# A dilated 3x3 convolution on one core: the first pair's load in one transfer, the later loads asked for five pairs ahead

## The chip, the core and the metric

The kernel runs on one core of one Trainium2 chip. The metric is device time in microseconds (us) of one execution. A measurement of this kernel repeats to about 1%: three runs of the kernel before lie between 126.32 and 127.67 us.

## What is computed

The reference is a 3x3 convolution with dilation 2 and zero padding 2, stride 1, on float32. Sixteen images of 64 channels and 64x64 pixels give sixteen images of 128 channels and 64x64 pixels:

```
x: (16, 64, 64, 64) f32, weight: (128, 64, 3, 3) f32, dilation = 2, pad = 2
for b, co, ci, kh, kw:
    output[b, co] += weight[co, ci, kh, kw] * x_pad[b, ci, kh*2 : kh*2+64, kw*2 : kw*2+64]
```

In bytes, x has 16.8 MB and the output 33.6 MB.

## The kernel before

**Tiles.** Two images share the 128 partitions (64 channels each): this is a pair, and there are `NP` = 8 of them. A pair's input is held as f16 in one of six `x16` buffers (`x16pool`, line 50). Because the dilation is 2, rows of the same parity interact; the kernel uses a sum of neighbouring row groups (`s16`, three buffers) to save multiplications: per unit `u` (16 output rows, four units a pair) TensorE makes three accumulations in PSUM, one from `s16` with the middle weights and two from `x16` with differences and outer weights (lines 203 to 213). ScalarE copies the first to `s32`, VectorE adds it to the other two and writes `o`, the pair's output in f32, 2 MB per image, 4 MB per pair.

**Buffers of outputs.** `opool` has three buffers (line 53). The first is taken at the start by `x32`, the f32 input of pair 0 (line 72); `o0` takes the second, `o1` the third, `o2` the first again, `o3` that of `o0`, `o4` that of `o1`, and so on. VectorE can't write `o4` until the output transfer of `o1` has landed.

**Inputs.** Pair 0 comes from SyncE's queue in f32, behind the weights, as rows 0 to 35 and rows 36 to 63 (lines 74 and 75), and is cast to f16 on VectorE (line 130) and ScalarE (line 132). Pairs 1 to 7 come through `load` (line 78), issued by GpSimd: a DMA that casts f32 to f16 on its way, 2.1 MB read and 1.05 MB written. `load(1)` is asked for between two subtractions on the weights (line 110). GpSimd also makes the row sums, `prepare` (line 135). For pair 0 it reads `x32`; `prepare(0, 0, 20)` (line 145) stands ahead of `load(2)`, `load(3)`, `load(4)` (lines 146 and 147).

**Order.** The order on each engine is that of the program text (`tc.manual_schedule()`). The main loop (line 190) runs over pairs and units; in unit 1 it asks for a load (line 195) and then for `prepare` of the next pair's rows 0 to 35, in unit 2 for rows 36 to 63. Engines run ahead as far as their waits allow, so GpSimd can be a pair or more ahead of TensorE: `prepare(pb + 1)` needs the `s16` buffer that pair `pb - 2` used, and the first pairs need none freed.

**Outputs.** SyncE issues one transfer of 4 MB for each of pairs 0 to 4 (line 221), two of 2 MB for pairs 5 and 6, and four of 1 MB for pair 7, each half a pair's rows of one image (line 224).

Of the kernel before, what the change touches and what calls it, by code (L numbers as in the profile page):

```python
# [10 lines left out]
def kernel(  # L11
# [7 lines left out]
    nc = tc.nc  # L19

    B, CI, H, W = x.shape
# [8 lines left out]
    NP = B // 2  # L30
# [29 lines left out]
    x_pair = x.rearrange("(nb two) c h w -> nb (two c) h w", two=2)  # L60
# [10 lines left out]
    cuts0 = [0, 20, 36, 52, H]  # L71
    x32 = opool.tile([P, 2, H, W], f32, tag="o", name="x32")[:, 0]
    x16[0] = x16pool.tile([P, H, W], f16, tag="x16", name="x16_0")
    for lo, hi in ((0, 36), (36, H)):
        nc.sync.dma_start(out=x32[:, lo:hi], in_=x_pair[0, :, lo:hi])


    def load(pb, cuts):
        x16[pb] = x16pool.tile([P, H, W], f16, tag="x16", name=f"x16_{pb}")
        for lo, hi in zip(cuts, cuts[1:]):  # L80
            nc.gpsimd.dma_start(out=x16[pb][:, lo:hi], in_=x_pair[pb, :, lo:hi])  # L81

    AHEAD = 5
# [16 lines left out]
    for name, a in (("w21", 2), ("w01", 0)):  # L100
        for u in range(2):
            eng = nc.vector if name == "w21" else nc.gpsimd
            eng.tensor_sub(  # L103
                out=w16[:, SLOT[name] * KW : (SLOT[name] + 1) * KW, u, :],
# [8 lines left out]
    for n, name in enumerate(("w1", "w21", "w0", "w01", "w2")):  # L113
        ps = cpool.tile([P, 2, NB], f32, tag="ps", name=f"wt{n}")
        k0 = SLOT[name] * KW
        for j in range(KW):
            nc.tensor.matmul(  # L117
                out=ps[:, 0, j * CO : (j + 1) * CO],
# [16 lines left out]
    def prepare(pb, lo, hi):  # L135
        if pb not in s16:
            s16[pb] = sumpool.tile([P, 2 * NQ, W], f16, tag="s16", name=f"s16_{pb}")
        src = (x16[pb] if pb else x32).rearrange("p (q e r) w -> p q e (r w)", e=2, r=2)
        dst = s16[pb].rearrange("p (q r) w -> p q (r w)", r=2)
        q0, q1 = lo // 4, hi // 4  # L140
        nc.gpsimd.tensor_add(  # L141
            out=dst[:, q0:q1], in0=src[:, q0:q1, 0, :], in1=src[:, q0:q1, 1, :]
        )
# [37 lines left out]
    def phase(pb, u, terms):  # L181

        ps = cpool.tile([CO, 2, NB], f32, tag="ps", name="ps")
        for pair in zip(*(conv(pb, hb, ps[:, hb], u, terms) for hb in range(2))):
            for m in pair:
                nc.tensor.matmul(**m)  # L186
        return ps

    BOTH = NP - 3
    for pb in range(NP):  # L190
        o = opool.tile([P, 2, H, W], f32, tag="o", name=f"o{pb}")
        ov = o.rearrange("p b (q e r) w -> p b q e (r w)", e=2, r=2)
        for u in range(NU):

            if u == 1 and AHEAD <= pb + 2 < NP:
                load(pb + 2, [0, H])
            if pb + 1 < NP:
                if u == 1:
                    prepare(pb + 1, 0, 36)
                elif u == 2:  # L200
                    prepare(pb + 1, 36, H)

            s32 = spool.tile([P, 2, NB], f32, tag="s32", name="s32")
            nc.scalar.copy(out=s32, in_=phase(pb, u, [("w1", 2, 0)]))  # L204
            for e, terms in enumerate(
                ([("w21", 1, 0), ("w0", 1, -1)], [("w01", 0, 0), ("w2", 0, 1)])
            ):
                ps = phase(pb, u, terms)
                nc.vector.tensor_add(  # L209
                    out=ov[:, :, u * UQ : (u + 1) * UQ, e, :],  # L210
                    in0=ps.rearrange("p b (q c) -> p b q c", c=QW),
                    in1=s32.rearrange("p b (q c) -> p b q c", c=QW),
                )

            step = NU // 2 if pb == NP - 1 else NU
            if (u + 1) % step == 0:
                fl = slice((u + 1 - step) * 4 * UQ, (u + 1) * 4 * UQ)
                if pb < BOTH:  # L220
                    nc.sync.dma_start(out=out_pair[pb], in_=o)
                else:
                    for hb in range(2):
                        nc.sync.dma_start(out=out[2 * pb + hb, :, fl], in_=o[:, hb, fl])
# [35 lines left out]
```

## Time and profile before

| what | value |
|---|---|
| time, median of 3 runs | 126.75 us (126.32 to 127.67) |
| profiled execution: span, first to last instruction | 124.3 us |
| TensorE matmul busy | 105.2 us (85%) |
| VectorE busy | 80.8 us (65%) |
| GpSimd busy | 41.4 us (33%) |
| HBM read, written | 17.07 MB, 33.55 MB |
| granted TensorE clock, mean | 0.965 |

The span is what the profiler saw between the first and the last instruction. The profile gives no device time of its own for the profiled execution; the three timed runs are 2.0 to 3.4 us longer than its span (126.32 and 127.67 less 124.3), the median 2.45 us. Those microseconds lie around the span. All places in time below are counted from the span's start. "Landing" is the last semaphore increment of a transfer; each transfer is split over 16 DMA engines, which finish one by one.

A load that casts is counted in the profile's GB/s with the bytes that it writes, half of those that it reads.

### The profile page before, as it was taken

The numbers are of one execution on the slowest core, as the hardware profiler recorded it, in microseconds if no ns is written. First come the engines' busy times: TensorE is split into PE (matmuls) and PEld (weight loads), VectorE is DVE, ScalarE is ACT, GpSimd is POOL, SyncE is SP. The second block draws the span as 40 slices with busy tenths as digits, with TensorE's granted clock in tenths as the row PEclk, the third lists the DMA queues.
The fourth block names the chain that finished last, engine by engine and source line by source line (L and its number), as shares of the span: only waits on it lengthen the run. The fifth ranks groups of instructions, "written<-read, shape, count | busy, mean of one in ns | idle before, by whom it ended". The sixth has DMA issues, their size and how long they took to land.

```text
span 124.3 us, 2244 instructions
## 1 busy us (share of the span) xinstructions
PE 105.2 (85%) x981; PEld 55.7 (45%) x981; DVE 80.8 (65%) x71; ACT 39.6 (32%) x40; POOL 41.4 (33%) x33
## 2 busy tenths in 40 slices
PE   6357999999999999999999999999999999960000
PEld 2043555555555555555555555555555555520000
DVE  0470199787778777877769778777877787770000
ACT  4760823333333333333333333333332433320000
POOL 2859998794095009500930093000000000000000
PEclk9999999999999999999999999999999999999655
DMA  4999999999999999999999999999999999999991
GB/s 129 346 359 218 214 214 216 224 237 411 393 327 314 332 306 319 316 390 314 324 345 427 425 427 432 422 427 427 432 438 427 432 414 432 427 417 419 422 406 71
DMA packets 3961, 43.42 MB, mean 349 GB/s; under 512 B 368, under 2 KB 368, under 8 KB 624
## 3 DMA queue, kind: packets, MB, share of 16 engines
q1 hardware_dynamic: 2944, 35.95, 68.9%
q0 software_dynamic: 1008, 7.34, 28.4%
q8 instruction: 7, 0.11, 0.3%
q14 instruction: 2, 0.02, 0.0%
HBM read 17.07 MB, written 33.55 MB: 407 GB/s over the span
## 4 chain that ended last, share of the span: by engine, by line
PE 80%; DMA 5%; POOL 2%; DVE 1%; DVEq 1%; SPq 0%; issue 0%
PE ps L186 80%; DMA x<-in_x_dram 5%; POOL s L141 2%; DVE o L209 1%; DVEq L255 1%; SPq L64 0%; DVEq L209 0%
## 5 line engine op out<-in xcount | busy, mean ns | idle before, releaser
L209 DVE TENSOR_TENSOR o<-ps,s 128x1024 f32<-128x1024 f32 x64 | 76.7, 1223 | 25.9 <-PE ps L186 16.8
L186 PE MATMUL ps<-x,w_sb 64*128 64x496 f16 (+3 forms) x768 | 85.3, 368 | 0.0
L186 PEld LDWEIGHTS <-w_sb 64*128 64x128 f16 x960 | 53.4, 95 | 49.3 <-issue 3.7
L204 ACT COPY s<-ps 128x1024 f32<-128x1024 f32 x32 | 32.4, 1012 | 63.0 <-PE ps L186 63.0
L141 POOL TENSOR_TENSOR s<-x 128x1152 f16<-128x1152 f16 (+4 forms) x18 | 35.1, 1971 | 31.1 <-PE ps L186 28.3
L186 PE MATMUL ps<-s,w_sb 64*128 64x496 f16 (+1 forms) x192 | 26.5, 379 | 2.1 <-POOL s L141 2.1
L81 POOL DMA_DIRECT2D x<-in_x_dram x7 | 4.0, 579 | 0.0
L132 ACT CAST x<-x 128x1024 f16<-128x1024 f32 (+1 forms) x3 | 2.8, 973 | 3.4 <-DMA x<-in_x_dram 3.4
L93 PE MATMUL warm<-zero 128*128 128x512 f16 x6 | 2.7, 630 | 1.2 <-DVE zero L87 1.2
L117 PE MATMUL wt<-ident,w 128*128 128x128 f16 x15 | 1.8, 312 | 2.1 <-ACT w L99 2.1
L103 DVE TENSOR_TENSOR w<-w 128x192 f16<-128x192 f32 x2 | 1.5, 800 | 2.5 <-DMA w<-in_weight_dram 2.5
L117 PEld LDWEIGHTS <-w 128*128 128x128 f16 x15 | 1.5, 146 | 3.0 <-ACT w L99 3.0
L99 ACT CAST w<-w 128x576 f16<-128x576 f32 x2 | 2.3, 1222 | 1.6 <-DMA w<-in_weight_dram 1.6
L103 POOL TENSOR_TENSOR w<-w 128x192 f16<-128x192 f32 x2 | 1.9, 951 | 2.4 <-DMA w<-in_weight_dram 2.4
L126 DVE CAST w_sb<-wt 128x384 f16<-128x384 f32 x3 | 1.6, 552 | 1.4 <-PE wt L117 1.4
L93 PEld LDWEIGHTS <-zero 128*128 128x128 f16 x6 | 0.7, 138 | 2.3 <-DVE zero L87 1.2
L99 ACT ACT_TABLE_LOAD x1 | 1.3, 1283 | 0.7 <-PEq L241 0.7
L128 ACT CAST w_sb<-wt 128x384 f16<-128x384 f32 x2 | 1.0, 478 | 1.1 <-PE wt L117 1.1
L130 DVE CAST x<-x 128x1280 f16<-128x1280 f32 x1 | 0.8, 826 | 0.5 <-DMA x<-in_x_dram 0.5
L87 DVE MEMSET zero<- 128x256 uint32 x1 | 0.3, 272 | 0.9 <-PEq L241 0.9
masks.py:199 POOL TENSOR_SCALAR_AFFINE_SELECT ident<-ident 128x128 f16<-128x128 f16 x1 | 0.3, 292 | 0.1
masks.py:197 POOL MEMSET ident<- 128x128 f16 x1 | 0.2, 204 | 0.3 <-POOLq L241 0.3
(4 smaller groups left out, 0.4 us busy)
## 6 DMA issues: line engine op xcount, KB each, us to landing
out_dram<-o SPq DMA_DIRECT2D x5, 4096.0 KB, 21.6
out_dram<-o SPq DMA_DIRECT2D x4, 2048.0 KB, 12.4
x<-in_x_dram POOLq DMA_DIRECT2D x7, 1024.0 KB, 16.0
out_dram<-o SPq DMA_DIRECT2D x4, 1024.0 KB, 10.6
x<-in_x_dram SPq DMA_DIRECT2D x1, 1152.0 KB, 6.5
x<-in_x_dram SPq DMA_DIRECT2D x1, 896.0 KB, 10.6
w<-in_weight_dram SPq DMA_DIRECT2D x1, 288.0 KB, 2.9
```

What stands on the lines that cost most here:

```text
L81: nc.gpsimd.dma_start(out=x16[pb][:, lo:hi], in_=x_pair[pb, :, lo:hi])
L93: nc.tensor.matmul(out=warm[:, 0], lhsT=zero[:, 0:P], rhs=zero, start=True, stop=True)
L99: nc.scalar.copy(out=w16[:, 0:NK, u, :], in_=w32k)
L103: eng.tensor_sub(out=w16[:, SLOT[name] * KW : (SLOT[name] + 1) * KW, u, :], in0=w32k[:, a * KW : (a + 1) * KW, :], in1=w32k[:, KW : 2 * KW ...
L117: nc.tensor.matmul(out=ps[:, 0, j * CO : (j + 1) * CO], lhsT=w16[:, k0 + j, :, :].rearrange("o t i -> o (t i)"), rhs=ident, start=True, st ...
L126: nc.vector.tensor_copy(out=dst, in_=ps[:, 0, 0 : KW * CO])
L132: nc.scalar.copy(out=x16[0][:, lo:hi], in_=x32[:, lo:hi])
L141: nc.gpsimd.tensor_add(out=dst[:, q0:q1], in0=src[:, q0:q1, 0, :], in1=src[:, q0:q1, 1, :])
L186: nc.tensor.matmul(**m)
L204: nc.scalar.copy(out=s32, in_=phase(pb, u, [("w1", 2, 0)]))
L209: nc.vector.tensor_add(out=ov[:, :, u * UQ : (u + 1) * UQ, e, :], in0=ps.rearrange("p b (q c) -> p b q c", c=QW), in1=s32.rearrange("p b ( ...
L255: with _tile.TileContext(nc) as tc:
```

## The change

The two transfers of pair 0 become one of whole rows, still on SyncE's queue behind the weights. In the main loop the load asked for in unit 1 of pair `pb` is that of pair `pb + 5` instead of `pb + 2`; since pairs 1 to 4 are asked for before the loop, loads 5, 6 and 7 now stand in pairs 0, 1 and 2 instead of 3, 4 and 5. Each still stands ahead of that unit's `prepare` on GpSimd. `load(6)` and `load(7)` go into the `x16` buffers of pairs 0 and 1.

```diff
     cuts0 = [0, 20, 36, 52, H]
     x32 = opool.tile([P, 2, H, W], f32, tag="o", name="x32")[:, 0]
     x16[0] = x16pool.tile([P, H, W], f16, tag="x16", name="x16_0")
-    for lo, hi in ((0, 36), (36, H)):
-        nc.sync.dma_start(out=x32[:, lo:hi], in_=x_pair[0, :, lo:hi])
+    nc.sync.dma_start(out=x32, in_=x_pair[0])
...
         for u in range(NU):
 
-            if u == 1 and AHEAD <= pb + 2 < NP:
-                load(pb + 2, [0, H])
+            if u == 1 and pb + AHEAD < NP:
+                load(pb + AHEAD, [0, H])
             if pb + 1 < NP:
                 if u == 1:
                     prepare(pb + 1, 0, 36)
```

## The prediction

> **What bounds the kernel now.** I read the page's slices first: is an engine full from end to end?
>
> ```profile
> PE   6357999999999999999999999999999999960000
> ...
> DMA  4999999999999999999999999999999999999991
> GB/s 129 346 359 218 214 214 216 224 237 411 393 327 314 332 306 319 316 390 314 324 345 427 425 427 432 422 427 427 432 438 427 432 414 432 427 417 419 422 406 71
> ```
>
> TensorE is full from slice 4 to slice 35, but the DMA engines are full from the second slice to the second last, and work four slices beyond TensorE. The GB/s only seem to vary. Where casting loads run alone (slices 3 to 7), 214 GB/s written are 428 read; outputs alone make 427 to 432; in between both run. So the rate is 428 to 430 GB/s throughout, whatever the mix. 17.07 + 33.55 = 50.62 MB at 430 are 117.7 us; the trace's packet records run from 1.74 to 122.9 us. Only about 3.5 us are lost, nearly all at the start.
>
> The chain of waits names TensorE for 80%, but look where it ends:
>
> ```profile
> 9.95 99.61 PE ps L186 x948
> ...
> 110.88 1.13 DVEq L255
> ```
>
> That is 112 us in a span of 124.3. What follows is the queue's drain, seen in SyncE's waits:
>
> ```profile
> SPq L255 <- DMA out_dram<-o: 9.2, 4, 2.4
> ```
>
> The last two output transfers are issued at 112.0 and 112.4 and land 8.9 and 10.9 us later; their 2.1 MB alone take 4.9 us. So some 5 us of older output are still queued when TensorE has done. **The DMA engines set the end.** TensorE has that much slack: the last two could be issued at about 117 (123.4, the last landing, less 4.9, less 0.5 for the landing and 1.0 from issue to first packet, which the weights show: issued 0.74, first packet 1.74).
>
> The stages say the same; the last two columns are DMA share and GB/s:
>
> ```profile
> 3.00:8.00 5.00, 2.72 (x18) 1.65 (x17) 2.40 (x4) 3.29 (x5) 2.83 (x4) 1.00 0.97 369
> 8.00:13.00 5.00, 3.05 (x16) 1.37 (x17) 1.44 (x3) 1.65 (x3) 5.00 (x6) 1.00 1.05 233
> 13.00:28.00 15.00, 15.00 (x148) 8.14 (x146) 11.48 (x10) 6.25 (x8) 13.69 (x8) 1.00 1.04 221
> ```
>
> Now the rule for this change: work only moved in the queue costs nothing, but time in which the queue is **empty** is lost in full. So I look for what keeps it fed at the start. GpSimd's timeline:
>
> ```profile
> 4.74 0.70 POOL L81 DMA_DIRECT2D x<-in_x_dram  x1
> 5.46 0.80 POOL L103 TENSOR_TENSOR w<-w 128x192 f16<-128x192 f32 x1
> 7.72 2.18 POOL L141 TENSOR_TENSOR s<-x 128x640 f16<-128x640 f32 x1 [1.47 <-DMA x<-in_x_dram]
> 9.84 1.63 POOL L81 DMA_DIRECT2D x<-in_x_dram  x3
> 11.46 7.63 POOL L141 TENSOR_TENSOR s<-x 128x512 f16<-128x512 f32 x5
> ```
>
> Load 1 is issued at 4.74; loads 2 to 4 at 9.84, behind prepare(0, 0, 20), which waited for the **first piece** of pair 0 (issued 1.17, landed 6.5 us later, 7.65). Load 1's packets run from 8.24 to 13.1 on most DMA engines and to 13.9 on the slowest (all landed at 14.7); load 2's packets follow from 13.25 without a hole.
>
> **Part one, the single transfer.** Removed: one DMA issue on SyncE (0.42 us), hidden, since nothing on that queue follows for 24 us. The packets: 9,216 bytes took 0.347 us and 7,168 bytes 0.272, in sum 0.619; one of 16,384 bytes takes 0.611 in the outputs. Eight per engine: 4.95 against 4.89 us, no gain.
>
> Moved: all that waits for rows 0 to 19 now waits for all 64. Landing: the slowest DMA engine ended its first piece at 7.33; eight packets of 0.28 bring it to 9.6, plus 0.3 to land (7.33 to 7.65): 9.9 at the earliest. On that engine load 1's packets come in between: the second piece landed only at 12.3. That is the late end. One packet of load 1 (0.62) in between gives 10.5, which I take: large packets leave fewer places to cut in.
>
> From there GpSimd's rows go on: prepare 2.2 us to 12.7, then load 2's issue. From a load's issue to its first packet I have three rows where the casting queue was empty: load 1, 4.74 to 8.24 (3.5 us); load 5, 28.77 to 33.34 (4.6); load 7, 50.73 to 55.23 (4.5). In all three other packets were already in the engines, so part may be waiting behind them; load 1's began on each engine just as the first pair's ended. Ends: 1.0 us (the weights' issue on idle engines, another queue) and 3.5. I take 2.7, nearest to the same queue's row, less a packet or two. So load 2's first packet comes at 10.5 + 2.2 + 2.7 = **15.4**, where load 1 ends at 13.1 to 14.0. The queue is empty for 1.4 us on the slowest DMA engine and 2.3 on the fastest. The last transfer's landings are also 2.5 us apart from engine to engine (120.9 to 123.4), so the fast ones can afford most of theirs; which engine is last at the end I can't tell from the start. I take **+1.7 us**. Ends: 9.9 + 2.2 + 1.0 = 13.1 gives 0; 12.3 + 2.2 + 3.5 = 18.0 gives +4.0.
>
> The Trainium skill, "DMA: Bandwidth & Descriptors", section "Latency and other measured facts", puts the first byte of a GpSimd-issued DMA at about 1 us; counted from the issue's end (0.55), load 2 would be ready at 14.3 and cost 0.3 us, an estimate from that page. The three rows above, 3.5 to 4.6 us, speak against it as far as they go.
>
> TensorE starts 2.85 us later (10.5 for 7.65): its first matmul waited for prepare(0, 0, 20). It ends at about 112.4 and issues its last outputs at 115.3, inside the limit of 117. Hidden; beyond it each microsecond would count in full.
>
> **Part two, loads 5 to 7 earlier.** GpSimd runs ahead already: these were issued at 28.8, 38.4 and 50.7. Now load 5 follows prepare(0) at about 17; load 6 waits for pair 0's last matmul (about 27) and load 7 for pair 1's (39.5), for their buffers. This wait is new. Behind it on GpSimd stand prepare(2) and prepare(3), 4.2 us each, done by 31.5 and 44, and TensorE wants them at about 38 and 50: free. The three issues take 0.57 us each as before.
>
> The queue's bytes are the same, so the drain isn't longer. But two early loads go ahead of outputs, and those free the `o` buffers:
>
> ```profile
> DVE o L209 <- DMA out_dram<-o: 1.2, 1, 1.2
> ```
>
> This is o4 waiting at 62.5 for o1's output, landed at 63.6. After: loads 0 to 7 and outputs 0 and 1 are all done at 65 + 1.7 = 66.7 (load 7's last packet today is at 65.8, about 1 us of output 2 among them), against a want of 62.5 + 2.85 = 65.4: a wait of about 1.3 us, as today. Output 0, mixed one to one with loads, lands near 50.5, wanted near 53.5. A wait here means a full queue and costs nothing until TensorE's slack is gone. Part two: **0**, between 0 and +1 (a wait 3 us longer, 115.3 to 118.3, 1.3 past the limit).
>
> **Sum.** 124.3 + 1.7 = 126.0 span; with the 2.45 around it, **128.4 us**.
>
> **Rivals.**
> No hole: load 2 is ready by 14, by a quick landing or a short issue. For it: the low ends. Against: 3.5 us is the shortest row of that queue. Time 126.75 (126.3 to 127.7).
> A larger hole: pair 0 lands at 12.3 as its second piece does today and the issue takes 3.5. +2.5 to +4, 129.3 to 130.8. Against: fewer, larger packets.
> Faster: the lag between DMA engines is made at the start (first piece 6.2 to 7.65 by engine, 1.45 us) and is there at the end (2.5). If whole rows of 16 KB bring the engines level, the slowest ends up to 1.4 us sooner: 125.3. It decides if the lag at load 1's landing shrinks by more than the hole. Against: the lag shows already in the weights (3.0 to 3.6), ahead of pair 0.
> One transfer saves the other's fixed cost: by rows it can't, for the second piece's packets follow the first's without a hole on each engine; if 2 us were saved, 124.7.
> The Trainium skill's fit (same page, section "Anatomy of one DMA — SWDGE (gpsimd) path") of 2.0 us for each transfer plus its bytes would say so, but for transfers one at a time; the trace has 0 between the pieces.
>
> **How the numbers follow.** Forecast 0.53 (own range 127.6 to 129.3), no hole 0.27, larger hole 0.13, faster by level engines 0.06, by the fixed cost 0.01. A measurement here can't tell less than 1% (1.3 us) from no change: slower is above 128.0, that is 0.85 of the forecast and all of the larger hole, 0.58; faster 0.07; within 0.35. The range takes in no hole and most of the larger: 126.2 to 130.2.
>
> **What would show it.** Right: prepare(0, 0, 20) starting near 10.5 and loads 2 to 4 issued near 12.7; a dip in the DMA row of slice 4 (12.4 to 15.5); the end of the drain later by the dip, TensorE's first matmul at 12.8. Wrong: no dip, or a dip that the drain doesn't show; TensorE ending past 117; a wait of VectorE for outputs of several us; the rate off 430 GB/s where loads and outputs mix.

## The result and the profile after

| | before | after |
|---|---|---|
| time, median of 7 runs each on one chip | 126.39 us | 127.81 us |
| ratio, 95% interval | | 1.0114 (1.0075 to 1.0153) |
| span of the profiled execution | 124.3 us | 126.1 us |
| end of the last DMA packet | 122.9 us | 124.8 us |

The changed kernel is slower by 1.1%, some 1.4 us. The forecast was 128.4 us with a span of 126.0; the size came out right. The profile after shows that only about half of the reason did; that the sum was right is luck in good part.

The page's slices of the changed kernel (3.15 us each; TensorE's busy tenths, the DMA engines' busy tenths, GB/s):

```profile
PE   6344999999999999999999999999999999980000
...
DMA  5999999999999999999999999999999999999991
GB/s 177 374 307 208 174 190 213 213 216 164 322 343 320 320 322 309 327 340 387 424 411 431 434 442 421 416 421 442 442 421 426 416 398 457 431 392 421 418 405 78
```

The DMA row has no dip, although one was forecast for slice 4. But the GB/s row has two that were not there: 174 and 190 in slices 4 and 5 (12.6 to 18.9 us), and 164 in slice 9 (28.4 to 31.5 us). In those slices only casting loads ran, and their usual figure is 213 to 216. The DMA engines were not empty there, they were slow.

GpSimd's timeline of the changed kernel shows why the forecast hole is missing:

```profile
4.63 0.70 POOL L80 DMA_DIRECT2D x<-in_x_dram  x1
5.35 0.80 POOL L102 TENSOR_TENSOR w<-w 128x192 f16<-128x192 f32 x1
8.84 2.18 POOL L140 TENSOR_TENSOR s<-x 128x640 f16<-128x640 f32 x1 [2.69 <-DMA x<-in_x_dram]
10.96 1.63 POOL L80 DMA_DIRECT2D x<-in_x_dram  x3
```

Pair 0 landed at 8.77, not at 10.5, and its landing was even over the DMA engines (8.14 to 8.77). Load 2 was issued at 10.96, not 12.7, and its first packet started at 13.04 by the trace's packet records, just as load 1 ended (13.0 to 13.8).

The stages tell the loss. First the kernel before, then the changed one, in the same window (the last two columns are DMA share and GB/s):

```profile
13.00:17.00 4.00, 4.00 (x40) 2.29 (x38) 1.97 (x2) 3.01 (x4) 4.00 (x3) 1.00 1.05 219
```

```profile
13.00:17.00 4.00, 4.00 (x29) 1.89 (x27) 1.66 (x2) 0.56 (x1) 3.98 (x5) 1.00 1.00 174
...
28.70:31.20 2.50, 2.50 (x26) 1.30 (x24) 1.75 (x3) 1.01 (x1) 2.50 (x2) 1.00 1.02 151
```

About the same share of busy time (1.05, 1.00 and 1.02), but a fifth fewer bytes in the first stage (174 for 219) and three tenths fewer in the second (151 where casting loads alone usually make 214; the kernel before was already writing outputs there). A packet of a casting load (16 KB read) usually takes 0.62 to 0.63 us. In these two stages many took 0.75 to 1.5 us.

To compare kernels, I add up over all packets what each took beyond the usual time of its size (0.618 us for a casting load's packet, a little under the commonest value, which adds the same 0.4 us or so to every kernel's sum; 0.611 for 16 KB of output, 0.347, 0.309, 0.272 and 0.09 for the smaller sizes) and divide by the 16 DMA engines. This is the **loss** in a stage, in us of the queue's time:

| stage | before | after |
|---|---|---|
| 0 to 8 us: weights and pair 0 | 0.86 | 0.63 |
| 8 to 12: load 1 takes over | 0.10 | 0.28 |
| 12 to 20: load 2 takes over (burst A) | 0.09 | 0.87 |
| 24 to 40: loads and outputs first run together (burst B) | 0.24 | 1.01 |
| all else | 0.70 | 0.77 |
| sum | 2.00 | 3.55 |

That is 1.55 us more. Besides, counting the DMA engines without a packet, the changed kernel had 0.16 us of empty queue between 10 and 15 us, and some 0.16 more than the kernel before between 100 and 105; the kernel before had none in the first and 0.06 in the second. 1.55 + 0.16 + 0.16 = 1.87 against the 1.9 us by which the last packet ended later. So close a match is partly chance: a second profile of the kernel before, below, ends 0.6 us later with the same loss.

### The profile page after: what moved, and what is told of

Its sections match the earlier page's. It is cut to its first block, busy times and chain, and to the rows that moved or that the text cites. A ratio compares the mean times of both kernels' runs of the same rounds, so it can differ in the third digit from the quotient of the medians.

```text
span 126.1 us, 2240 instructions
## 1 busy us (share of the span) xinstructions
PE 106.1 (84%) x981; PEld 56.0 (44%) x981; DVE 80.9 (64%) x71; ACT 39.7 (31%) x40; POOL 41.5 (33%) x33
## 4 chain that ended last, share of the span: by engine, by line
PE 55%; DMA 28%; DVE 4%; POOL 2%; DVEq 1%; issue 0%; SPq 0%
PE ps L185 55%; DMA out_dram<-o 22%; DMA x<-in_x_dram 6%; DVE o L208 4%; POOL s L140 2%; DVEq L254 1%; SPq L64 0%; DVEq L208 0%
## 5 line engine op out<-in xcount | busy, mean ns | idle before, releaser
L185 PE MATMUL ps<-x,w_sb 64*128 64x496 f16 (+3 forms) x768 | 86.2, 370 | 0.3 <-DVE o L208 0.3
```

## The experiments

In the expectations, "burst A" and "burst B" are the two places of the table, and each theory stands under its letter. All ratios are against the kernel before on the same chip.

**1. Each part alone, both again, and loads 2 to 4 ahead of the wait.**

The first part alone (`a1_one_transfer`):

```diff
-    for lo, hi in ((0, 36), (36, H)):
-        nc.sync.dma_start(out=x32[:, lo:hi], in_=x_pair[0, :, lo:hi])
+    nc.sync.dma_start(out=x32, in_=x_pair[0])
```

> The first part alone: pair 0 in one transfer, loads 5 to 7 where they were. In the changed kernel the end came 1.9 us later, though the queue had no hole: the packets of load 2 (13 to 17 us) and of load 5 (28.7 to 31.4 us) took 0.75 to 1.5 us each for 0.62, in sum 0.85 and 0.8 us per DMA engine. Theory P (each part has its own burst): load 2's burst belongs to the single transfer, load 5's to the early loads; here +0.8 to +1.0 us and slow packets only in load 2. Theory L (bursts come from the early loads' place alone): 0. Theory S (the single transfer does it all, by bringing the engines level): +1.4 us, the whole. Theory X (disturbance from outside, another place each time): no fixed place.

Measured: 1.0109 (1.0067 to 1.0151). Burst A 0.58 and, where load 5 joins output 0 at 33 to 35 us, a burst that brings stage 24 to 40 to 0.84. Theory L (0 here) falls, and theory P, which had no second burst here, fails in that part. Theory S has the time right here.

The second part alone (`a2_loads_early`):

```diff
-            if u == 1 and AHEAD <= pb + 2 < NP:
-                load(pb + 2, [0, H])
+            if u == 1 and pb + AHEAD < NP:
+                load(pb + AHEAD, [0, H])
```

> The second part alone: two pieces of 36 and 28 rows as before, loads 5 to 7 five pairs ahead. Theory P: slow packets only in load 5 (near 27 to 30 us, as output 0 begins), +0.5 to +0.8 us. Theory L: +1.4 us. Theory S: 0. Theory X: no fixed place.

Measured: 1.0048 (1.0027 to 1.0070). No burst A (0.09); stage 24 to 40 loses 0.85. Theory S, which had 0 here, falls. The window in which output 0, issued at 25.04, waits for its first packet at 29.02, while load 4 ends and load 5 (first packet 28.09) begins:

```profile
26.70:29.00 2.30, 2.30 (x24) 1.20 (x22) 1.55 (x3) 1.01 (x1) 2.30 (x2) 1.00 1.03 160
```

160 where casting loads alone usually make 214.

The changed kernel again, nothing edited (`a3_both_again`):

> The changed kernel once more, for a second profile of it. Theories P, L and S: the slow packets lie again at 13 to 17 and at 28.7 to 31.4 us, time +1.4 us. Theory X: they lie elsewhere or are gone in the profile.

Measured: 1.0122 (1.0083 to 1.0160). The bursts lie where they lay: A is smaller (0.29), B the same (1.03). So theory X falls, and A's size varies from one execution to the next. **The two parts don't add up**: 1.1% and 0.5% alone, 1.1 to 1.2% together. With either part alone there is one burst B, and with both there is still one.

The changed kernel with the later loads ahead of the wait (`a4_loads_first`):

```diff
-    prepare(0, 0, 20)
     for pb in range(2, AHEAD):
         load(pb, [0, H])
+    prepare(0, 0, 20)
```

> The changed kernel with loads 2, 3 and 4 issued ahead of prepare(0, 0, 20), near 6.2 us instead of 11, so that they are queued long before load 1 ends. The prediction's theory (the queue runs short since load 2 is asked for late): the loss of load 2's stage goes, +0.4 to +0.6 us in place of +1.4. Theory S: no change, +1.4. If slow packets stay in load 2 at 13 to 17 us, the lateness of its issue is not their cause.

Measured: 1.0069 (1.0029 to 1.0109). Issued at 6.12, load 2 has no burst (stage 12 to 20: 0.10), and the window that had 174 GB/s in the changed kernel has the usual 213:

```profile
13.00:17.00 4.00, 4.00 (x26) 1.82 (x22) 1.23 (x1) 1.01 (x1) 3.98 (x5) 1.00 1.02 213
```

So burst A needs the late issue. The time is 0.9 us over the kernel before, more than the 0.4 to 0.6 expected, and its interval overlaps that of the changed kernel. Stage 8 to 12 rises to 0.49, burst B stays (0.89). In this execution pair 0 landed at 9.7, TensorE's work came later, and the queue ran dry late:

```profile
100.50:103.00 2.50, 2.50 (x30) 1.51 (x28) 2.08 (x3) 1.01 (x1) 0.00 (x0) 1.00 0.74 311
```

A DMA share of 0.74: pair 5's outputs had drained before pair 6's were issued at 102.54. The DMA engines stood empty for 0.79 us here. So TensorE's later start is hidden only just in the changed kernel, and not wholly in this run.

**2. Are the bursts the change's, and which part makes which?**

The kernel before once more, for its profile alone (`b1_before_again`):

> The kernel before once more, for a second profile. So far the kernels with one transfer or with early loads show two bursts of slow packets: burst A in load 2 (13 to 17 us; 0.25 to 0.75 us lost per DMA engine) and burst B for some 2 us where the loads' queue and the outputs' queue first run together (0.6 to 0.85 us lost); the first profile of the kernel before shows neither. Theory F (the bursts come from the change): again neither, under 0.15 us in each place. Theory C (chance of the one profile): burst B here too.

Measured: again neither burst (stages 0.10, 0.09, 0.25). But its last packet ended at 123.5 for 122.9, with the same loss: from one execution to the next the slowest DMA engine's end varies by 0.6 us, which bounds how well such a sum can close.

The kernel before with loads 2 to 4 late (`b2_late_loads`):

```diff
-    prepare(0, 0, 20)
+    for lo, hi in zip(cuts0[:3], cuts0[1:]):
+        prepare(0, lo, hi)
     for pb in range(2, AHEAD):
         load(pb, [0, H])
-    for lo, hi in zip(cuts0[1:], cuts0[2:]):
-        prepare(0, lo, hi)
+    prepare(0, 52, H)
```

> The kernel before, still with two pieces and late loads 5 to 7, but loads 2 to 4 issued behind prepare of rows 0 to 51, near 11 us as in the changed kernel instead of 8.4 to 9.8. Theory J (burst A is load 2's packets made just in time, as load 1 ends at 13): burst A appears, 0.25 to 0.75 us lost at 13 to 17, time +0.3 to +0.7 us. Theory S (the single transfer makes burst A): no burst, time 0 to +0.2.

Measured: 1.0060 (1.0026 to 1.0094). Loads issued at 11.81; the first packet of load 2 at 13.29, 1.5 us later, and then burst A, 0.58:

```profile
13.00:15.00 2.00, 2.00 (x24) 0.99 (x20) 2.00 (x2) 0.24 (x1) 2.00 (x3) 1.00 0.96 147
```

The kernel before has 205 GB/s in that window. Burst A needs no single transfer: theory S falls here too, J holds. And a burst B came unasked (stage 24 to 40: 0.84): load 4 now begins 0.7 us later (23.77 for 23.03) and ends later, so output 0, issued at 24.82, finds it running and gets its first packet only at 29.05. The moment of issue alone doesn't decide it: in `b1_before_again` output 0 was issued at 24.85, also with load 4 running, waited 3.0 us until load 4 ended, and there was no burst.

The single transfer with the loads first (`b3_one_first`): the edits of `a1_one_transfer` and `a4_loads_first`, loads 5 to 7 late as before.

> The single transfer with loads 2 to 4 issued ahead of prepare(0, 0, 20), loads 5 to 7 late as before: neither the late issue of load 2 nor the early loads. Theory J: burst A gone; what is left is the handover from pair 0 to load 1 near 8 us (0.3 to 0.5 lost) and burst B if the single transfer makes that (0.6): +0.4 to +1.0 us. If both bursts come from the late issue alone: 0 to +0.2 us.

Measured: 1.0071 (1.0024 to 1.0117). Burst A gone (0.09), stage 8 to 12 at 0.64, burst B where load 5 joins output 0 (0.91).

The single transfer alone once more, for its profile alone (`b4_one_again`):

> The single transfer alone, once more, for a second profile. Theory F: burst A at 13 to 17 us and burst B where load 5 joins output 0 (33 to 35 us, 0.6 us lost in the first profile) again. Theory C: burst B may be missing.

Measured: both bursts again (0.58 and 1.07). Theory F holds.

**3. What makes burst B with a single transfer?**

The kernel before with the loads first (`c1_two_first`): the edit of `a4_loads_first` on the kernel before.

> The kernel before with loads 2 to 4 issued ahead of prepare(0, 0, 20), at about 6.3 us; two pieces, loads 5 to 7 late. It differs from the one-transfer kernel with loads first (+0.7%) only in the pieces. Theory K (the single transfer makes the burst where load 5 joins output 0): no burst at 33 to 35 us, time within 0.2 us of the kernel before. Theory M (the burst is paid by the first time that the two queues run together, however pair 0 came): burst of 0.6 us there unless output 0 meets load 4 first; +0.5 us.

Measured: 0.9991 (0.9974 to 1.0008), no burst in either place (0.10 and 0.21). Beside `b3_one_first`, which differs only in pair 0's pieces, this is what the single transfer costs when the loads come early: some 0.8% (1.0071 against 0.9991, whose intervals don't overlap). Theory M falls and theory K holds here. The windows of the two, first `c1_two_first`, then `b3_one_first`:

```profile
33.00:35.20 2.20, 2.20 (x24) 1.10 (x22) 1.78 (x2) 0.97 (x1) 0.90 (x1) 1.00 0.99 331
```

```profile
33.00:35.20 2.20, 2.20 (x26) 1.12 (x22) 1.45 (x3) 0.48 (x1) 0.00 (x0) 1.00 1.04 279
```

One more small transfer behind pair 0, in the single-transfer kernel with loads first (`c2_one_first_extra`) and in the kernel before (`c3_two_extra`):

```diff
+    scratch = wpool.tile([CO, 64], f32, name="scratch")
+    nc.sync.dma_start(out=scratch, in_=weight.rearrange("o i h w -> o (i h w)")[:, 0:64])
```

> The single transfer with loads 2 to 4 first and loads 5 to 7 late, and behind pair 0 on the same queue one more small transfer (64 columns of the weights to a scratch tile that nothing reads, 32 KB), so that SyncE's queue has as many descriptors as with two pieces. Theory N (the burst hangs on where in the queue's ring the descriptors lie): burst at 33 to 35 us gone, +0.1 to +0.3 us. Theories K and M: burst of 0.6 to 0.8 us stays, +0.7 to +1.0 us.

> The kernel before with the same small extra transfer behind its two pieces. Theory N: a burst may appear where the queues first run together, up to +0.7 us. Theories K and M: none, within 0.2 us.

Measured: 1.0112 (1.0091 to 1.0133) and 1.0058 (1.0038 to 1.0079). In the first, burst B stays (1.03): the number of transfers on SyncE's queue isn't its cause, theory N falls. The second lost 0.87 in stage 24 to 40, against the forecast of theories K and M. Theory N had allowed a burst there, but this one needs no N: TensorE was earlier, output 0 was issued at 22.85, just ahead of load 4's first packet (23.16), and load 4's packets were slow at 25 to 26 us, before output 0's began at 27.04, as in `a2_loads_early` and `b2_late_loads`. When load 5 joined later, there was no second burst. This run also had some 0.4 us of empty queue between 100 and 105 us.

**4. Does TensorE's time matter at all?** The changed kernel without one of three taps (`d1_less_matmul`):

```diff
-    KWS = (1, 0, 2)
+    KWS = (1, 0)
...
-        n, total = 0, len(terms) * KW
+        n, total = 0, len(terms) * len(KWS)
```

> The changed kernel without the right-hand tap of each row of the filter: a third of the convolution's matmuls left out, so the output lacks those products; every transfer is the same. Theory of the prediction (the DMA engines set the end and TensorE is hidden): within 1.5 us of the changed kernel, 126.3 to 129.3 us, although TensorE has some 30 us less to do. If TensorE sets the end: 100 to 110 us.

Measured: 1.0129 (1.0078 to 1.0180), against 1.0114 for the changed kernel with all its taps; in time 127.80 and 127.81 us. From this kernel's page, TensorE's first line and the DMA engines' slices:

```profile
PE 81.1 (64%) x661; PEld 38.2 (30%) x661; DVE 77.4 (61%) x71; ACT 39.8 (32%) x40; POOL 41.6 (33%) x33
...
DMA  5999999999999999999999999999999999999990
```

and its waits:

```profile
DVE o L208 <- DMA out_dram<-o: 15.1, 2, 8.1
...
PE ps L185 <- DVE o L208: 14.6, 2, 7.8
```

A third of the matmuls gone, 25 us less of busy TensorE (81.1 for 106.1), and not a microsecond gained: much of that time turned into waits for output transfers.

**Losses side by side** (us per DMA engine; "joins" is what met a running queue in stage 24 to 40):

| kernel | pieces | load 2 issued | 8 to 12 | 12 to 20 | 24 to 40 | joins | ratio |
|---|---|---|---|---|---|---|---|
| before | 2 | 9.84 | 0.10 | 0.09 | 0.24 | load 5 to output 0 | 1 |
| b1_before_again | 2 | 9.28 | 0.10 | 0.09 | 0.25 | load 5 to output 0 | profile only |
| c1_two_first | 2 | 6.20 | 0.29 | 0.10 | 0.21 | load 5 to output 0 | 0.9991 |
| a2_loads_early | 2 | 8.40 | 0.13 | 0.09 | 0.85 | output 0 to load 5 | 1.0048 |
| b2_late_loads | 2 | 11.81 | 0.12 | 0.58 | 0.84 | output 0 to load 4 | 1.0060 |
| c3_two_extra | 2 | 8.30 | 0.18 | 0.10 | 0.87 | output 0 to load 4 | 1.0058 |
| a1_one_transfer | 1 | 10.95 | 0.44 | 0.58 | 0.84 | load 5 to output 0 | 1.0109 |
| b4_one_again | 1 | 11.66 | 0.28 | 0.58 | 1.07 | load 5 to output 0 | profile only |
| b3_one_first | 1 | 6.30 | 0.64 | 0.09 | 0.91 | load 5 to output 0 | 1.0071 |
| c2_one_first_extra | 1 | 6.22 | 0.43 | 0.10 | 1.03 | load 5 to output 0 | 1.0112 |
| a4_loads_first | 1 | 6.12 | 0.49 | 0.10 | 0.89 | output 0 to load 5 | 1.0069 |
| after | 1 | 10.96 | 0.28 | 0.87 | 1.01 | output 0 to load 5 | 1.0114 |
| a3_both_again | 1 | 10.99 | 0.35 | 0.29 | 1.03 | output 0 to load 5 | 1.0122 |
| d1_less_matmul | 1 | 11.14 | 0.47 | 0.39 | 1.37 | output 0 to load 4 | 1.0129 |

Two rules fit every row. Loads issued at 10.95 or later have burst A (0.29 to 0.87), loads issued at 9.84 or earlier don't. Where output 0 joins a running load, stage 24 to 40 loses 0.84 to 1.37; where its first packet comes as load 4 ends and load 5 joins later, it loses 0.21 to 0.25 with two pieces and 0.84 to 1.07 with one. Why pair 0's pieces matter for what happens at 33 us **stays open**: the runs rule out the number of transfers on the queue and the lateness of loads 2 to 4, no more. What the DMA engines do during a burst isn't in the profile either.

## Why the prediction was right, and where it wasn't

**The DMA engines set the end: right.** The kernel without a third of its matmuls takes the same time. The queue's time is what counts, and the 1.87 us of slow packets and empty queue match the 1.9 us by which it ends later, within the 0.6 us between two profiles of one kernel. One reading was off: the 3.5 us lost in the kernel before are not "nearly all at the start". By the packets some 1.1 us go before 8 us and about as much after 111 us, where the DMA engines end one by one.

**The landing of pair 0: mis-sized.** The term was 10.5 us, measured 8.77, below the low end of 9.9. The slowest DMA engine had been taken as 1.3 us behind the fastest, as in the profile before; with one transfer the engines were within 0.63 us. Part of that is chance: in the five other executions with two pieces the first piece had landed by 6.75 to 7.18 (7.65 in the profile on which the forecast rests) and the second by 8.96 to 9.91 (12.29 there); one transfer landed at 8.76 to 9.71 in eight. Level engines were part of the rival "faster by level engines", and indeed stages 0 to 8 lost 0.23 us less; it doesn't pay for the rest. The larger hole and the saved fixed cost are out: pair 0 landed early, and the time rose.

**From a load's issue to its first packet: mis-sized.** The term was 2.7 us. Measured: 2.1 us (10.96 to 13.04), and 1.5 in the kernel with late loads (11.81 to 13.29). So the rest of the 3.5 to 4.6 us in the rows before was probably waiting behind packets already in the engines, which no run separates, and the low end was the better choice. The first byte about 1 us after the issue that the Trainium skill states ("DMA: Bandwidth & Descriptors", section "Latency and other measured facts") agrees with the run with late loads: 11.81 plus 0.55 us of issue to 13.29 is 0.9 us. In the changed kernel it is 1.5 us.

**The hole: wrong in kind, and half right in place.** The sum gave an empty queue of 1.4 to 2.3 us between load 1 and load 2; by the terms as measured (8.77 + 2.19 to load 2's issue + 2.08 = 13.04) it hardly opens, 0.16 us. By the prediction's own signs the hole is refuted: no dip in slice 4, prepare(0, 0, 20) at 8.84 for 10.5, TensorE's first matmul after it at 11.07 for 12.8. The rival "no hole" had this right, but concluded no change. What neither had: a load issued so late that it is only just in time costs nearly as much as a small hole. Its packets are slow for some microseconds, 0.78 us more than before in this profile. With loads 2 to 4 issued at 6.1 that loss is gone.

**"Part two: 0": wrong alone, right on top of part one, by luck.** It rested on a rate of 428 to 430 GB/s "whatever the mix". That holds in the steady state. It fails when one queue joins another in flight: the early loads alone cost 0.48%, and stage 24 to 40 of the changed kernel loses 0.77 us more than before. Before, output 0 came at 27.7, just as load 4 ended; now load 5 is in flight. The profile before couldn't show this price, for it has no such meeting. As a term added to part one, 0 is what was measured (1.0109 with part one alone, 1.0114 with both), but only because part one brings a burst B of its own, which part two moves rather than adds. A bound from both sides of zero was owed here; the +1 given was for another mechanism.

**The waits and places of part two: right.** Loads 5, 6, 7 were issued at 15.96, 26.43 and 38.80 (forecast 17, 27, 39.5). Output 1 landed at 66.77 (66.7). VectorE waited for it longer than the 1.3 us forecast:

```profile
DVE o L208 <- DMA out_dram<-o: 2.5, 1, 2.5
```

TensorE lost some 0.4 us by it: its units run 1.81 us behind those of the kernel before at 16 us (16.35 for 14.54) and 2.24 at the end (109.71 for 107.47). The last outputs were issued at 114.7 (115.3).

**TensorE hidden: right, but by less than told.** The limit of 117 us was worked out for the last two outputs. The tighter place is earlier: pair 6's outputs, issued at 101.99, came as pair 5's ran out. The changed kernel's window there:

```profile
100.50:102.50 2.00, 2.00 (x24) 1.13 (x20) 1.59 (x3) 1.01 (x1) 0.00 (x0) 1.00 0.89 365
```

A share of 0.89 goes with the 0.16 us of empty queue in the sum above; with TensorE half a microsecond later still (`a4_loads_first`, issue at 102.54) it was 0.79 us.

So the forecast of +1.7 us was met by 0.78 of burst A, 0.77 of burst B, 0.18 at load 1, 0.32 of empty queue, less 0.16 elsewhere (0.23 won at the start, 0.07 lost in the rest): the right size, from a hole that hardly opened and two losses that the prediction did not have. Burst A shares the hole's place and its cause, load 2's late issue. Burst B was not foreseen at all, and that the two add up to the forecast is luck.

## What to carry to other kernels

When the DMA engines are full from end to end, moving a transfer is not free: look at what it meets. Read the GB/s row next to the busy row, since a full engine can move a quarter less (160 for 214 GB/s here), and ask of every load whether it is queued well before its predecessor ends (here 9.8 us was early enough, 10.95 was not, for a predecessor ending at 13 to 14) and whether it will be in flight when the other queue's first large transfer comes. Take a landing from more than one execution before building on it. And check an engine's slack at every hand-over to the bound resource, not only at the last one.

## What the runs showed of the hardware

- Casting loads and outputs run together in the steady state at full rate, but output 0 joining a running load got its first packet 4.0 to 4.2 us after its issue in most runs (25.04 to 29.02, 24.82 to 29.05, 27.26 to 31.40), and in the last 2 us or so of that the running load's packets took 0.75 to 1.6 us for 0.62: 0.6 to 0.8 us lost in all (1.1 in `d1_less_matmul`), beside the 0.2 that this stage loses anyway. Issued as the load ended, it had its first packet after 0.9 us (27.52 to 28.43, `a1_one_transfer`); issued 2.2 to 3.0 us before the load's end, it waited for that end with no burst (25.45 to 27.69 in the kernel before, 24.85 to 27.88 in `b1_before_again`). In the runs with a burst more of the loads was still ahead (load 4 itself, or load 5 queued behind it); why that matters is open.
- The price was paid once: of loads 6 and 7, which also ran beside outputs, none brought another burst.
- One transfer of whole rows landed by 8.76 to 9.71 us in eight executions. Two pieces had landed in full by 8.96 to 9.91 us in five executions and at 12.29 in the first profile, the one with a late DMA engine. So the gain for the last rows is under 1 us as a rule, and the first rows, which landed at 6.75 to 7.65, come later.
